# A gated MLP on one core of Trainium2: fifteen pairs of weight tiles by seven products in chains of up to five, and the norm's factor of the value side applied behind the output product

## The chip, the cores and the metric

The kernel runs on one core of a Trainium2 chip. The metric is the time of one execution on the device in microseconds (us); less is better. The engines of the core work in parallel, each on its own list of instructions: PE (TensorE) multiplies matrices into PSUM, DVE (VectorE), ACT (ScalarE) and POOL (GpSimd) work elementwise, and SP (SyncE) starts DMAs.

## What is computed

The model has two transformer blocks, 512 tokens of width 1024 and, in the first, 16 meta tokens more (528 columns). The first block has a layer of differential attention and one of latent attention, the second a mixer of a convolution and windowed attention. Each of these three layers is followed by a gated MLP, and the MLPs are what is changed:

```python
def conv_ffn(h, g_norm, w_in, conv_w, conv_b, w_out):
    L = h.shape[1]
    xn = rms_norm(h, g_norm)
    a, b = jnp.split(xn @ w_in, 2, axis=-1)
    ap = jnp.pad(a, ((0, 0), (CONV_W - 1, 0), (0, 0)))
    a_conv = conv_b
    for j in range(CONV_W):
        a_conv = a_conv + ap[:, j:j + L] * conv_w[j]
    return h + (jax.nn.silu(a_conv) * b) @ w_out
```

`rms_norm` multiplies each token by a factor R of its own, 1/sqrt(mean of squares + eps), and each channel by a gain. The MLP of the second block is the same in other names. The width between `w_in` and `w_out` is 2816, 22 tiles of 128. Everything is fp32.

## The kernel before

Activations lie transposed: channels on partitions, tokens along the columns. An fp32 operand is kept as a high and a low part of the type that PE multiplies, and a product is three matmuls: weight high by input high, weight high by input low, weight low by input high (`lin`, L329). The high part of weights is a cast on ACT (L162, `whi`), the low part a subtraction on DVE (L170) or, for some, on POOL (L112), both `wlo`. `Xh` and `Xl` are the parts of a layer's input `h` times its gain (L426 to L430), without R, which is a factor of a token and is applied behind the product.

**The MLP** (`ffn`, called three times; below MLP 1 to 3). Gate tile f and value tile NF+f make a pair. A pair runs in one of two ways. `Plain` makes both tiles by the 8 slices of the input's channels in two column halves: 2 x 8 x 2 x 3 = 96 matmuls. `Seven` makes the pair by seven products instead of eight, on sums and differences of halves of the weights and of the input: 7 blocks of 4 slices x 3 = 84 matmuls of H columns (264, 258 and 256 in MLP 1, 2 and 3). The sums of the input (`T`) are made once per MLP (`differences`), those of the weights for each pair by eight POOL additions of 128x256 (`combine`); they come from two loads (`raw`, `rawA`) and give four sets of weights, a, s, t and d. The sums overwrite `raw` and `rawA`, and the last set, d, is split from there by POOL, so that a buffer of `rawA` (two of them) is free for a later pair's load only when d is split.

Behind the products a pair goes on as follows. The gate side is multiplied by R, into `am` (L608 for a Plain; L672 for a Seven, whose sums go by L660, L666 and L670). `gate` does the convolution over three tokens (ACT, then two DVE instructions at L561) and SiLU, and **L565 multiplies the result by R**: that is R of the value side. L618 (Plain) or L678 (Seven) multiplies by the value product, and `split` puts the result as `Gh` and `Gl` into G.

**Groups.** The 22 pairs are taken in four groups (`GROUPS`: first pair, end, steps). A number among the steps is a Plain by itself; a tuple is a run of one or two Sevens whose products are mixed with those of the one Plain that stands last in it (`turns`). Per MLP that makes 12 Sevens and 10 Plains. After each group `group_h` multiplies the group's part of G by that part of `w_out`, for eight tiles `m` of output channels, and adds the result `po` to `h`: one DVE instruction that reads PSUM and SBUF (`add`, L693). MLP 1 does it in two column halves of 272 and 256, MLP 2 and 3 in one of 512. The last group's product leads into the next layer: `add_h` (L447) adds to `h`, takes the squares for the next norm (ACT into a ring of two buffers named `sq`, then sums `acc` and, behind MLP 2, `gacc`, on POOL but for the last), and makes `Xh` and `Xl` of the next layer. In MLP 3 `finish` does it, with the final norm and the output.

**What sets the order.** In `opening` (pair 0) and in the tuples PE's order is the order of the code (`in_order`). Otherwise, and on the other engines, a scheduler puts independent instructions in order when the program is built. Weights are taken from a plan (`plan_ffn`) in the order of use; `Weights.get` loads three sets ahead and splits two ahead. `tp` holds the working tiles of an MLP, `am` with two buffers, and six PSUM banks (`psp`) take the products.

## Time and profile before

| | |
|---|---|
| median of three runs | 2083.66 us (2083.62 to 2084.5) |
| the profiled execution | 2083.53 us, its span 2081.7 us |
| PE busy | 2041.2 us, 98% of the span |
| DVE busy | 1395.4 us, 67% |
| ACT busy | 975.1 us, 47% |
| POOL busy | 737.8 us, 35% |
| the chain that ended last | 82% PE, 12% DVE, 3% ACT |
| mean granted clock of TensorE | 0.995 of full speed |

The profile is of one execution. Its span runs from the first to the last recorded instruction; 1.8 us of the execution's time lie around it. "Busy" counts the time in which an engine works on at least one instruction; neighbouring DVE instructions overlap a little in the records, so that a mean duration is somewhat longer than the distance from start to start. The chain that ended last goes back from the last instruction to whatever released each step: where it runs through PE, matmuls took the time, where it runs through DVE, PE waited or would soon have waited for DVE.

### The profile page before, as it was taken

To read this page: it belongs to the slowest core of one execution; us is meant where nothing else is said; L and a number is where in the kernel's file an instruction comes from. 1 tells how busy PE (TensorE), PEld (TensorE's weight loads), DVE (VectorE), ACT (ScalarE), POOL (GpSimd) and SP (SyncE) were. 2 spreads that over 40 slices of the span, in tenths; PEclk is the share of its full clock that TensorE was granted. 3 is DMA by queue.
4 is the path that set the end of the run, shared out by engine and by line. 5 is a ranking of instruction groups with operands and counts; after the bars stand their busy time and mean duration, and the time that the engine had idled before them with its cause. 6 is when DMAs were issued, how large, how long until landed. Compare 5 with 4: busy or idle time off the path is not lost.

```text
span 2081.7 us, 36278 instructions
## 1 busy us (share of the span) xinstructions
PE 2041.2 (98%) x14327; PEld 1888.2 (91%) x14327; DVE 1395.4 (67%) x2536; ACT 975.1 (47%) x1940; POOL 737.8 (35%) x837
## 2 busy tenths in 40 slices
PE   8999999999999999999999999999999999999998
PEld 7999899999999989899899998788888889899997
DVE  8787769576767476658676768675533358577675
ACT  6565546344445455545344445354432235344444
POOL 5223243445343231124445453321122244435442
PEclk9999999999999999999999999999999999999999
DMA  5111132323322211022323323322223232323322
GB/s 170 52 54 59 42 103 76 97 86 104 102 79 82 68 41 42 31 88 73 114 80 104 93 94 93 92 81 78 70 76 102 97 117 69 104 85 108 112 71 72
DMA packets 56426, 174.91 MB, mean 84 GB/s; under 512 B 6464, under 2 KB 9408, under 8 KB 56256
## 3 DMA queue, kind: packets, MB, share of 16 engines
q1 hardware_dynamic: 55824, 172.34, 26.2%
q8 instruction: 112, 1.84, 0.4%
q14 instruction: 58, 0.48, 0.1%
q10 hardware_dynamic: 432, 0.27, 0.0%
HBM read 170.45 MB, written 2.10 MB: 83 GB/s over the span
## 4 chain that ended last, share of the span: by engine, by line
PE 82%; DVE 12%; ACT 3%; issue 1%; POOL 1%; DMA 1%; SPq 0%; ACTq 0%; DVEq 0%; POOLq 0%
PE po L329 22%; PE pf L552 17%; PE pf L329 13%; PE pc L329 5%; PE pq L329 5%; PE pg L329 4%; DVE wlo L170 3%; PE s L743 2%; PE pyc L329 2%; PE pm L329 2%; PE pd L329 2%; PE o L1383 1%; PE pya L329 1%; ACT whi L162 1%; PE pt L1361 1%
## 5 line engine op out<-in xcount | busy, mean ns | idle before, releaser
L162 ACT CAST whi<-raw 128x1024 fp32r<-128x1024 f32 (+4 forms) x460 | 382.0, 840 | 548.0 <-PE po L329 172.7
L112 POOL TENSOR_TENSOR wlo<-raw,whi 128x256 fp32r<-128x256 f32 (+1 forms) x336 | 291.9, 896 | 569.9 <-ACT whi L162 565.2
L170 DVE TENSOR_TENSOR wlo<-raw,whi 128x512 fp32r<-128x512 f32 (+2 forms) x580 | 398.6, 725 | 53.8 <-ACT whi L162 51.2
L329 PE MATMUL pf<-Xl,whi 128*128 128x256 f32 (+2 forms) x960 | 271.3, 283 | 0.9 <-DVE Xl L430 0.9
L329 PE MATMUL pf<-Xh,whi 128*128 128x256 f32 (+2 forms) x960 | 271.5, 283 | 0.0
L329 PE MATMUL pf<-Xh,wlo 128*128 128x256 f32 (+2 forms) x960 | 271.3, 283 | 0.0
L329 PE MATMUL po<-Gh,wlo 128*128 128x512 f32 (+2 forms) x709 | 238.8, 339 | 0.0
L329 PE MATMUL po<-Gl,whi 128*128 128x512 f32 (+2 forms) x709 | 238.5, 337 | 0.0
L329 PE MATMUL po<-Gh,whi 128*128 128x512 f32 (+2 forms) x709 | 235.7, 340 | 0.0
L329 PEld LDWEIGHTS pf<-Xl,whi 128*128 128x128 f32 x960 | 181.4, 189 | 1.2 <-DVE Xl L430 1.1
L329 PEld LDWEIGHTS pf<-Xh,whi 128*128 128x128 f32 x960 | 181.6, 189 | 0.0
L329 PEld LDWEIGHTS pf<-Xh,wlo 128*128 128x128 f32 x960 | 181.5, 189 | 0.0
L552 PE MATMUL pf<-Th,whi 128*128 128x264 f32 (+2 forms) x576 | 162.5, 282 | 0.3 <-DVE bm L666 0.3
L552 PE MATMUL pf<-Tl,whi 128*128 128x264 f32 (+2 forms) x576 | 162.3, 282 | 0.0
L552 PE MATMUL pf<-Th,wlo 128*128 128x264 f32 (+2 forms) x576 | 162.3, 282 | 0.0
L329 PEld LDWEIGHTS po<-Gh,wlo 128*128 128x128 f32 x709 | 133.2, 188 | 16.7
L329 PEld LDWEIGHTS po<-Gl,whi 128*128 128x128 f32 x709 | 133.4, 188 | 15.3
L329 PEld LDWEIGHTS po<-Gh,whi 128*128 128x128 f32 x709 | 132.4, 188 | 14.8
L693 DVE TENSOR_TENSOR h<-po,h 128x272 f32<-128x272 f32 (+1 forms) x96 | 53.6, 560 | 108.6 <-PE po L329 108.1
L552 PE MATMUL pf<-Xh,whi 128*128 128x264 f32 (+2 forms) x432 | 122.0, 282 | 2.6 <-DVE ct L618 2.6
L552 PE MATMUL pf<-Xh,wlo 128*128 128x264 f32 (+2 forms) x432 | 121.9, 282 | 0.0
L552 PE MATMUL pf<-Xl,whi 128*128 128x264 f32 (+2 forms) x432 | 121.8, 282 | 0.0
(425 smaller groups left out, 5568.8 us busy)
## 6 DMA issues: line engine op xcount, KB each, us to landing
raw<-in_w_in_dram SPq DMA_DIRECT2D x134, 512.0 KB, 3.6
raw<-in_w_up_dram SPq DMA_DIRECT2D x44, 512.0 KB, 3.3
raw<-in_w_qkv_dram SPq DMA_DIRECT2D x24, 512.0 KB, 3.6
raw<-in_w_out_dram SPq DMA_DIRECT2D x32, 384.0 KB, 3.1
raw<-in_w_out_dram SPq DMA_DIRECT2D x32, 320.0 KB, 2.9
raw<-in_w_o_dram SPq DMA_DIRECT2D x16, 512.0 KB, 3.4
raw<-in_w_dn_dram SPq DMA_DIRECT2D x16, 384.0 KB, 3.3
raw<-in_w_dn_dram SPq DMA_DIRECT2D x16, 320.0 KB, 2.9
```

The costliest lines, as they stand in the source:

```text
L112: self.net.nc.gpsimd.tensor_tensor(d[:, c], a[:, c], b[:, c], op=op)
L162: nc.scalar.copy(h[:, c0 : c0 + z], r)
L170: nc.vector.tensor_tensor(l[:, c], r[:, a:b], h[:, c].bitcast(F32), op=ALU.subtract)
L329: nc.tensor.matmul(ps, w, x, start=first and i == 0, stop=i == len(ops) - 1, skip_group_check=not first)
L552: nc.tensor.matmul(ps[:, :H], a, b, start=first and i == 0, stop=i == len(ops) - 1, skip_group_check=not first)
L693: nc.vector.tensor_tensor(self.h[:, m, s:e], p, self.h[:, m, s:e], op=ALU.add)
L743: nc.tensor.matmul(s[:, :w], qa[:, q0 : q0 + P], ka[:, k0:k1], start=z == 0, stop=z == len(ops) - 1 and not masked,)
L1361: nc.tensor.transpose(t[:, b * P : (b + 1) * P], p[:, j, a : a + P], self.ident)
L1383: nc.tensor.matmul(o[:, i, j, :], st[n, "pt", j][:, b * P : (b + 1) * P], V[:, b, c], start=n % 4 == j == b == 0, stop=False,)
```

## The change

There are two parts.

*Chains.* `GROUPS` now names for each group the single Plains ahead of it, the Sevens, and one Plain for the end. `chain` takes the place of `turns`: the first Seven's products 1, 5, 6, 2, then for each next Seven y, with x the one ahead of it, the order y1 x7 x3 y5 x4 y6 y2, and after the last the Plain, whose gate half is put around the last Seven's products 7, 3 and 4. Per MLP there are 15 Sevens and 7 Plains, in chains of 2, 4, 5 and 4 Sevens. `plan_ffn` follows that order, and the record of sums (`rows`) is kept by name, not in a queue.

*The factor R of the value side.* L565 goes. Since R belongs to a token, and a token is a column of the output product too, the output product is multiplied by it instead: in `add`, DVE writes `po` times R to a tile `pr` in the ring `am`, and POOL adds that to `h`; in `add_h` and `finish`, `scaled` writes it to a tile in the ring `sq`, and DVE adds it to `h`. R of the gate side stays where it was.

```diff
-    (0, 6, (0, 1, 2, (3, 4, 5))),
-    (6, 11, ((6, 7, 8), (9, 10))),
-    (11, 17, ((11, 12, 13), (14, 15, 16))),
-    (17, 22, ((17, 18, 19), (20, 21))),
+    (0, 6, (0, 1, 2), (3, 4), 5),
+    (6, 11, (), (6, 7, 8, 9), 10),
+    (11, 17, (), (11, 12, 13, 14, 15), 16),
+    (17, 22, (), (17, 18, 19, 20), 21),
 )
...
 
     def plan_ffn(self, wi, wo):
         pl = []
-        for k0, k1, steps in GROUPS:
-            for st in steps:
-                if isinstance(st, int):
-                    pl += [self.chunk(wi, st), self.chunk(wi, NF + st)]
-                    continue
-                *fs, g = st
-                a, d = [[self.chunk(wi, m + f)[1] for f in fs] for m in (0, NF)]
-                u = [
-                    [((wi, f, "a"), a[i] + d[i], 8, P, "a"), ((wi, f, "s"), [], 8, P, "s")]
-                    + [((wi, f, "t"), [], 8, P, "t"), ((wi, f, "d"), [], 4, P, "d")]
-                    for i, f in enumerate(fs)
-                ]
-                wa, wb = self.chunk(wi, g), self.chunk(wi, NF + g)
-                if len(u) == 1:
-                    pl += [*u[0][:2], wa, u[0][2], wb, u[0][3]]
-                else:
-                    pl += [*u[0][:2], wa, u[0][2], u[1][0], u[0][3], u[1][1], wb, *u[1][2:]]
+        for k0, k1, front, sevens, g in GROUPS:
+            pl += [self.chunk(wi, f + z) for f in front for z in (0, NF)]
+            units = [
+                [((wi, f, "a"), [self.chunk(wi, m)[1][0] for m in (f, NF + f)], 8, P, "a")]
+                + [((wi, f, c), [], 4 if c == "d" else 8, P, c) for c in "std"]
+                for f in sevens
+            ]
+            pl += units[0][:2]
+            for x, y in zip(units, units[1:]):
+                pl += [y[0], x[2], y[1], x[3]]
+            pl += [self.chunk(wi, g), *units[-1][2:], self.chunk(wi, NF + g)]
...
-    def add_h(self, ps, m, s, e, gain=None):
+    def add_h(self, ps, m, s, e, gain=None, R=None):
 
         nc = self.nc
         hs = self.h[:, m, s:e]
         last = m == KD - 1
+        ps = ps if R is None else self.scaled(ps, R[:, s:e])
         nc.vector.tensor_tensor(hs, ps, hs, op=ALU.add)
         self.sq_add(self.acc, hs, s, e, m == 0, last)
         if gain is not None:
...
         self.split(*self.X.at(m, s, e), self.h[:, m, s:e], g)
+
+    def scaled(self, ps, r):
+        t = self.nrm.tile([P, 512], F32, tag="sq", name=self.n("pr"))[:, : ps.shape[-1]]
+        self.nc.vector.tensor_tensor(t, ps, r, op=ALU.mult)
+        return t
 
     def begin_h(self, pool, tag, name, X, halves, m, hf, k0=0, k1=KD - 1):
 
...
                 nc.scalar.activation(t, t, AF.Silu)
-                nc.vector.tensor_tensor(t, t, R[:, t0:], op=ALU.mult)
                 return t
 
             def bank(first=False):
...
-            def turns(k0, *fs):
-
-                u = [Seven(f, f - k0) for f in fs[:-1]]
-                v = Plain(fs[-1], fs[-1] - k0)
-                x, y = u[0], u[-1]
-                x.p1(), x.p5(), v.a(0), x.p6(), x.p2(), v.a(1), x.p7()
-                if x is y:
-                    v.b(0), x.p3(), x.p4(), v.b(1)
-                    return
-                x.p3(), y.p1(), x.p4(), y.p5(), y.p6(), y.p2(), v.b(0), y.p7(), y.p3(), v.b(1), y.p4()
+            def chain(k0, fs, g):
+
+                u = [Seven(f, f - k0) for f in fs]
+                v = Plain(g, g - k0)
+                x = u[0]
+                x.p1(), x.p5(), x.p6(), x.p2()
+                for y in u[1:]:
+                    y.p1(), x.p7(), x.p3(), y.p5(), x.p4(), y.p6(), y.p2()
+                    x = y
+                v.a(0), x.p7(), x.p3(), v.a(1), x.p4(), v.b(0), v.b(1)
 
             def add(p, m, s, e):
-                nc.vector.tensor_tensor(self.h[:, m, s:e], p, self.h[:, m, s:e], op=ALU.add)
+                t = tp.tile([P, NT], F32, tag="am", name=self.n("pr"))[:, : e - s]
+                nc.vector.tensor_tensor(t, p, R[:, s:e], op=ALU.mult)
+                nc.gpsimd.tensor_tensor(self.h[:, m, s:e], t, self.h[:, m, s:e], op=ALU.add)
 
             R = self.nrm.tile([P, NT], F32, tag="R", name=self.n("R"), bufs=1)
             with self.in_order():
                 opening()
             differences()
-            for k0, k1, steps in GROUPS:
-                for st in steps:
-                    if st == 0:
-                        continue
-                    if isinstance(st, int):
-                        v = Plain(st, st - k0)
+            for k0, k1, front, sevens, g in GROUPS:
+                for f in front:
+                    if f:
+                        v = Plain(f, f - k0)
                         v.a(0, 2), v.b(0, 2)
-                    else:
-                        with self.in_order():
-                            turns(k0, *st)
+                with self.in_order():
+                    chain(k0, sevens, g)
                 if k1 < NF:
                     self.group_h(psp, wo, G, k0, k1 - k0, ranges, add)
             xcx.close()
             if nxt is None:
-                self.finish(psp, wo, G, k0, k1 - k0)
+                self.finish(psp, wo, G, k0, k1 - k0, R)
                 return
             nxt()
-            self.group_h(psp, wo, G, k0, k1 - k0, ranges, lambda p, m, s, e: self.add_h(p, m, s, e, gain))
+            self.group_h(psp, wo, G, k0, k1 - k0, ranges, lambda p, m, s, e: self.add_h(p, m, s, e, gain, R))
 
 
     def rope(self, dst, src, rows, C, S, mask, pool, s=0, e=NT):
...
                 hs = self.h[:, m, META:]
-                nc.vector.tensor_tensor(hs, ps, hs, op=ALU.add)
+                nc.vector.tensor_tensor(hs, self.scaled(ps, R[:, META:]), hs, op=ALU.add)
...
                 hs = self.h[:, m, s:e]
-                nc.vector.tensor_tensor(hs, ps, hs, op=ALU.add)
+                nc.vector.tensor_tensor(hs, self.scaled(ps, R[:, s:e]), hs, op=ALU.add)
```

Where the instructions stand now is seen in the order of each engine. **First, DVE behind the last group of MLP 1.** `h<-po` and, after the change, `pr<-po` and `h<-pr` are the adds, `Xl` the low part of the next layer's input, `wlo` the splitting of weights. Before:

```order
L447 TENSOR_TENSOR h<-po_8185,h 128x272 [waits PE_49]
L447 TENSOR_TENSOR h<-po_8186,h 128x256 [waits PE_49]
L447 TENSOR_TENSOR h<-po_8233,h 128x272 [waits PE_49]
L170 TENSOR_TENSOR wlo_8278<-raw_0_8231,whi_8277 128x320 [waits DMAHW1_49,Activation_49]
L170 TENSOR_TENSOR wlo_8278<-raw_0_8231,whi_8277 128x320
L447 TENSOR_TENSOR h<-po_8234,h 128x256 [waits PE_49]
L427 TENSOR_TENSOR Xl_8177<-h,Xh_8176 128x272 [waits DVE_49,Activation_49]
L447 TENSOR_TENSOR h<-po_8284,h 128x272 [waits PE_49]
L427 TENSOR_TENSOR Xl_8177<-h,Xh_8176 128x256 [waits DVE_49,Activation_49]
```

After:

```order
L453 TENSOR_TENSOR pr_8329<-po_8297,R_3999 128x272 [waits PE_49]
L453 TENSOR_TENSOR pr_8335<-po_8298,R_3999 128x256 [waits PE_49]
L442 TENSOR_TENSOR h<-pr_8329,h 128x272 [waits DVE_49]
L442 TENSOR_TENSOR h<-pr_8335,h 128x256 [waits DVE_49]
L170 TENSOR_TENSOR wlo_8397<-raw_0_8346,whi_8396 128x320 [waits DMAHW1_49,Activation_49]
L170 TENSOR_TENSOR wlo_8397<-raw_0_8346,whi_8396 128x320
L453 TENSOR_TENSOR pr_8380<-po_8348,R_3999 128x272 [waits DVE_49,PE_49]
L421 TENSOR_TENSOR Xl_8289<-h,Xh_8288 128x272 [waits Activation_49]
L421 TENSOR_TENSOR Xl_8289<-h,Xh_8288 128x256 [waits DVE_49,Activation_49]
L442 TENSOR_TENSOR h<-pr_8380,h 128x272 [waits DVE_49]
L453 TENSOR_TENSOR pr_8388<-po_8349,R_3999 128x256 [waits DVE_49,PE_49]
L442 TENSOR_TENSOR h<-pr_8388,h 128x256 [waits DVE_49]
```

Each add has become two instructions, a product with R from PSUM and an add of two SBUF tiles; the `Xl` of a tile stands behind both.

**Second, DVE behind the last group of MLP 2**, its last tiles. `acc` and `gacc` are the running sums of squares. Before:

```order
L447 TENSOR_TENSOR h<-po_15754,h 128x512 [waits PE_49]
L430 SCALAR_TENSOR_TENSOR Xl_15556<-h,gg,Xh_15555 128x512 [waits Activation_49]
L170 TENSOR_TENSOR wlo_15870<-raw_0_15784,whi_15869 128x512 [waits DMAHW4_49,Activation_49]
L170 TENSOR_TENSOR wlo_15870<-raw_0_15784,whi_15869 128x512
L430 SCALAR_TENSOR_TENSOR Xl_15556<-h,gg,Xh_15555 128x512 [waits Activation_49]
L447 TENSOR_TENSOR h<-po_15786,h 128x512 [waits PE_49]
L1662 CAST bandb<-band 128x256 [waits Pool_49]
L430 SCALAR_TENSOR_TENSOR Xl_15556<-h,gg,Xh_15555 128x512 [waits Activation_49]
L353 TENSOR_TENSOR acc<-acc,sq_15803 128x512 [waits Activation_49]
```

After (from three tiles ahead of the end):

```order
L453 TENSOR_TENSOR pr_15954<-po_15938,R_11977 128x512 [waits Pool_49]
L442 TENSOR_TENSOR h<-pr_15954,h 128x512 [waits DVE_49]
L424 SCALAR_TENSOR_TENSOR Xl_15762<-h,gg,Xh_15761 128x512 [waits DVE_49,Activation_49]
L453 TENSOR_TENSOR pr_15988<-po_15972,R_11977 128x512 [waits Pool_49]
L442 TENSOR_TENSOR h<-pr_15988,h 128x512 [waits DVE_49]
L424 SCALAR_TENSOR_TENSOR Xl_15762<-h,gg,Xh_15761 128x512 [waits DVE_49,Activation_49]
L453 TENSOR_TENSOR pr_16022<-po_16006,R_11977 128x512 [waits PE_49,Pool_49]
L442 TENSOR_TENSOR h<-pr_16022,h 128x512 [waits DVE_49]
L347 TENSOR_TENSOR acc<-acc,sq_16025 128x512 [waits Activation_49]
L347 TENSOR_TENSOR gacc<-gacc,sq_16028 128x512 [waits Activation_49,Pool_49]
L424 SCALAR_TENSOR_TENSOR Xl_15762<-h,gg,Xh_15761 128x512 [waits DVE_49,Activation_49]
```

The products with R wait for POOL (the ring `sq` that they share with the squares), and the last `Xl` has moved behind the last adds into `acc` and `gacc`.

**Third, POOL in the group from pair 11 on in MLP 1**, where weights of Sevens are summed. The number behind a name is that of the set of weights. `raw` and `rawS` are sums, `wlo` a split. Before:

```order
L112 TENSOR_TENSOR wlo89_6562<-raw84_1_6309,whi89_6561 128x256 [waits PE_49,Activation_49]
L112 TENSOR_TENSOR wlo89_6562<-raw84_1_6309,whi89_6561 128x256
L112 TENSOR_TENSOR raw90_0_6566<-raw90_0_6566 128x256 [waits Pool_49]
L112 TENSOR_TENSOR rawS94_6749<-raw94_1_6727 128x256 [waits DMAHW1_49]
L112 TENSOR_TENSOR rawS94_6749<-raw94_1_6727 128x256
L112 TENSOR_TENSOR raw94_1_6727<-raw94_0_6725,raw94_1_6727 128x256 [waits DMAHW0_49,Pool_49]
L112 TENSOR_TENSOR raw94_1_6727<-raw94_0_6725,raw94_1_6727 128x256 [waits Pool_49]
L112 TENSOR_TENSOR wlo95_6846<-raw90_1_6568,whi95_6845 128x256 [waits PE_49,Activation_49]
L112 TENSOR_TENSOR raw94_0_6725<-rawS94_6749,raw94_0_6725 128x256 [waits DVE_49,Pool_49]
```

After, inside the chain:

```order
L113 TENSOR_TENSOR wlo91_6592<-raw84_1_6306,whi91_6591 128x256 [waits PE_49,Activation_49]
L113 TENSOR_TENSOR wlo91_6592<-raw84_1_6306,whi91_6591 128x256
L113 TENSOR_TENSOR rawS92_6637<-raw92_1_6598 128x256 [waits DMAHW7_49,DVE_49]
L113 TENSOR_TENSOR rawS92_6637<-raw92_1_6598 128x256
L113 TENSOR_TENSOR raw92_1_6598<-raw92_0_6596,raw92_1_6598 128x256 [waits DMAHW5_49,DVE_49,Pool_49]
L113 TENSOR_TENSOR raw92_1_6598<-raw92_0_6596,raw92_1_6598 128x256 [waits Pool_49]
L113 TENSOR_TENSOR raw92_0_6596<-rawS92_6637,raw92_0_6596 128x256 [waits DVE_49,Pool_49]
L113 TENSOR_TENSOR raw92_0_6596<-rawS92_6637,raw92_0_6596 128x256 [waits Pool_49]
L113 TENSOR_TENSOR raw92_0_6596<-raw92_0_6596 128x256 [waits DVE_49,Pool_49]
```

Before, the splits of a Plain's or another set's weights lay between two Sevens' sums; now each Seven's eight sums stand directly behind the split of the d set (`wlo<-raw`) of the Seven two ahead of it, and wait for DMAs into the buffers that this split sets free.

## Rows read from the trace of the kernel before

**Rows 1.** The page, busy us of each engine (share of the span, instructions).
```profile
PE 2041.2 (98%) x14327; PEld 1888.2 (91%) x14327; DVE 1395.4 (67%) x2536; ACT 975.1 (47%) x1940; POOL 737.8 (35%) x837
```
**Rows 2.** Windows: length, then PE, PEld, DVE, ACT, POOL busy (instructions), clock, DMA, GB/s.
```profile
555.00:590.50 35.50, 35.50 (x293) 35.50 (x293) 18.36 (x33) 9.38 (x15) 13.04 (x16) 1.00 0.34 105
651.37:680.06 28.69, 28.68 (x236) 28.47 (x234) 28.03 (x73) 22.93 (x69) 12.91 (x15) 1.00 0.40 128
683.20:686.50 3.30, 3.30 (x17) 3.30 (x16) 0.90 (x4) 0.78 (x3) 0.00 (x0) 0.52 0.38 103
1277.90:1307.00 29.10, 26.63 (x110) 20.76 (x109) 28.48 (x35) 20.74 (x32) 20.86 (x18) 0.96 0.38 119
```
**Rows 3.** Windows over eleven stretches of 84 matmuls of one Seven: sum and mean.
```profile
sum 110.41, PE 110.41 PEld 110.41 DVE 103.05 ACT 76.56 POOL 52.96; mean PE 10.04 PEld 10.04 DVE 9.37 ACT 6.96 POOL 4.81
```
**Rows 4.** The chain that ended last: start, us, a run of matmuls (MLP 1, MLP 3).
```profile
352.49 10.15 PE pf L552 x84
...
1760.59 9.89 PE pf L552 x84
```
**Rows 5.** DVE by line and shape, 651.37:680.06: count, busy, mean ns; idle before.
```profile
L427 DVE TENSOR_TENSOR Xl<-h,Xh 128x256 fp32r<-128x256 f32 x8 | 4.3, 543 | 0.0
```
**Rows 6.** Timeline of DVE and POOL behind MLP 1: start, us, instruction [idle before].
```profile
667.38 0.99 DVE L427 TENSOR_TENSOR Xl<-h,Xh 128x256 fp32r<-128x256 f32 x1
...
672.42 0.42 DVE L427 TENSOR_TENSOR Xl<-h,Xh 128x256 fp32r<-128x256 f32 x1
672.76 0.42 DVE L447 TENSOR_TENSOR h<-po,h 128x256 f32<-128x256 f32 x1
...
666.42 1.66 POOL L353 TENSOR_TENSOR acc<-acc,sq 128x256 f32<-128x256 f32 x2 [1.52 <-ACT sq L351]
```
**Rows 7.** By line and shape, 1277.9:1307, DVE, POOL and ACT: columns as in Rows 5.
```profile
L430 DVE SCALAR_TENSOR_TENSOR Xl<-h,gg,Xh 128x512 fp32r<-128x512 f32 x8 | 11.6, 1465 | 0.6 <-ACT Xh L429 0.6
L170 DVE TENSOR_TENSOR wlo<-raw,whi 128x512 fp32r<-128x512 f32 x6 | 6.2, 1078 | 0.0
L447 DVE TENSOR_TENSOR h<-po,h 128x512 f32<-128x512 f32 x8 | 5.4, 674 | 0.0
...
L353 POOL TENSOR_TENSOR acc<-acc,sq 128x512 f32<-128x512 f32 x5 | 7.4, 1487 | 11.1 <-ACT sq L351 11.1
L353 POOL TENSOR_TENSOR gacc<-gacc,sq 128x512 f32<-128x512 f32 x4 | 6.6, 1660 | 0.9 <-ACT sq L351 0.9
L112 POOL TENSOR_TENSOR wlo<-raw,whi 128x256 fp32r<-128x256 f32 x6 | 5.8, 989 | 0.0
...
L351 ACT ACTIVATE sq<-h 128x512 f32<-128x512 f32 x6 | 3.7, 617 | 0.0
L351 ACT ACTIVATE sq<-h,par 128x512 f32<-128x512 f32 x5 | 3.6, 715 | 1.1 <-POOL gacc L353 1.1
```
**Rows 8.** The chain that ended last, behind MLP 2: the step of one add.
```profile
1279.98 0.60 DVE h L447
```
**Rows 9.** By line and shape, 491:590.5 in MLP 1, DVE and POOL: columns as in Rows 5.
```profile
L170 DVE TENSOR_TENSOR wlo<-raw,whi 128x512 fp32r<-128x512 f32 x26 | 19.0, 772 | 2.1 <-ACT whi L162 1.7
...
L565 DVE TENSOR_TENSOR ct<-ct,R 128x528 f32<-128x528 f32 x6 | 4.7, 775 | 1.9 <-ACT ct L564 1.9
...
L112 POOL TENSOR_TENSOR wlo<-raw,whi 128x256 fp32r<-128x256 f32 x18 | 17.8, 1015 | 17.7 <-ACT whi L162 17.7
L112 POOL TENSOR_TENSOR raw<-rawS,raw 128x256 f32<-128x256 f32 x8 | 7.6, 969 | 4.5 <-DVE wlo L170 4.5
...
L112 POOL TENSOR_TENSOR raw<-raw,raw 128x256 f32<-128x256 f32 x8 | 6.2, 791 | 15.0 <-DMA raw<-in_w_in_dram 15.0
```
**Rows 10.** Timeline of DVE in MLP 1: one split, POOL idle from 503.9 to 508.4.
```profile
504.38 0.68 DVE L170 TENSOR_TENSOR wlo<-raw,whi 128x512 fp32r<-128x512 f32 x1
```
**Rows 11.** Waits of PE over the whole execution: us in total, times, longest.
```profile
PE pf L552 <- DVE ct L618: 2.6, 2, 1.8
```
**Rows 12.** The page, DMA issues: KB each, median us from issue to landing.
```profile
raw<-in_w_in_dram SPq DMA_DIRECT2D x134, 512.0 KB, 3.6
```

21 lines of the change are left out of this document (10 added, 11 removed).

## The prediction

> **What bounds the kernel now.** I read the busy shares first: PE works 98% of the span, DVE 67%, POOL 35% [rows 1]. Then stretches of single stages. Inside the three MLPs PE has no gap at all: over an output product (the first of [rows 2]), and over eleven stretches in which one pair by seven products (a Seven, 84 matmuls) runs by itself [rows 3], PE is busy for the whole time. There a matmul taken away is time taken away. DVE is close behind, though: 9.37 of 10.04 us in the Seven stretches, with POOL at 4.81 beside it. Two stages are the other way round. After the last group of MLP 1 DVE is busy 28.03 of 28.69 us, and after that of MLP 2 28.48 of 29.10 [rows 2]; both are the exits, where DVE adds the product to `h`, makes the low half `Xl` of the next layer's input and splits weights. The next layer's first product needs the last `Xl`, so there DVE sets the time, and PE runs on at a granted clock of 0.52, the lower of its two levels (1.2 of 2.4 GHz), when it has stood waiting (the third of [rows 2]). So the change is weighed twice: PE's saving inside the MLPs, and DVE's added work at the exits.
>
> **What PE saves.** Nine of 66 pairs change from 96 matmuls to 84. The 84 take 10.15 us in MLP 1 and 9.89 in MLP 3 [rows 4], MLP 2 lies between; 12 matmuls are 1.45 to 1.41 us, nine times 1.43 is **-12.9 us**. All of it is in stretches where PE never waits, so it counts in full if nobody becomes late.
>
> **The exit of MLP 1.** The gate's multiplication by R goes, but 16 products with R are added where DVE has no room. A DVE instruction of this size takes 0.42 us, and the next starts 0.34 after it (second and third of [rows 6]): 16 x 0.35 = 5.6. The 16 adds into `h` now read two SBUF operands, not PSUM and SBUF, as the `Xl` subtraction does. That form takes 0.543 on average here against 0.42 undisturbed [rows 5, 6], because of POOL: at 667.38 it took 0.99 while POOL was running, at 672.42 0.42 while it was not [rows 6]; 16 x 0.12 = 1.9. In PE's order 42 matmuls of this product, not 56, stand ahead of the end of its first tile, 14 x 0.12 = 1.7 earlier. Nothing else of PE can fill in behind the last `Xl`. Together **+5.6 us** (3.9 with undisturbed adds; 8.0 if the adds stretch to 0.99 for the 45% of the time in which POOL runs, 16 x 0.45 x 0.57 = 4.1 in place of 1.9).
>
> The Trainium skill (GPSIMD Engine Reference, 1. Specifications) says that GpSimd shares its SBUF interfaces with VectorE and that the two contend when a DVE instruction has two SBUF inputs. By that rule the trace agrees, 0.99 against 0.42, and the rule speaks against this change: it turns PSUM-and-SBUF adds into SBUF-and-SBUF adds at the exits and gives POOL more work elsewhere. Without it the exit would be 3.9.
>
> **The exit of MLP 2.** Eight products 512 wide are added; DVE's step for this size is 0.60 [rows 8], so at least 4.8. But the products take tiles of the ring of two buffers in which the squares for POOL's two running sums lie, and from the third on they wait for POOL. Behind each stand DVE's add, the `Xl`, and the weights' splitting. Per tile three allocations now pass two buffers, so the next square for `acc` needs the buffer that POOL's `gacc` add frees. A lap is at least `gacc` 1.66 + square 0.62 + `acc` 1.49 = 3.8; POOL's other work of this stretch (six splits at 0.99 [rows 7], and what is left of its 20.86 [rows 2]) adds some 0.9 per lap, so 4.7. Seven laps are 33. After the last come product 0.6, add 0.67, squares 0.62 and 0.72, the `gacc` add 0.7, now ahead of the last `Xl` on DVE, and `Xl` 1.47: 4.8. That is 37.8 where 29.1 stood: **+8.7 us** (4.8 to 10.5).
>
> **The end.** MLP 3 goes out through `finish`, where one more DVE product stands in the last chain: 0.42 as in rows 6, **+0.5**.
>
> **The openings.** PE waits 2.6 us on `ct` of the first pairs [rows 11]. Three gate multiplications fewer stand ahead of that (3 x 0.775 per MLP, [rows 9]), so up to 2.6 can go. Against it, the first chain is (3,4) without a Plain in between and asks for its second unit 8.8 us sooner. Preparing a unit takes its load, 3.6 [rows 12], eight sums on POOL at 0.79 to 0.97 and two splits at 1.0 [rows 9], 9.1 in all: a loop of 12.7 where a unit lasts 10.0 on PE. One missed turn per MLP is 2.7, three 8. **-1 us** (-2.6 to +8); most of what PE waits for there is the differences and the splits, which stay.
>
> **The chains.** Two things decide whether PE stays without gaps in the nine chains.
> DVE: a unit costs 9.37 now [rows 3], less one R multiplication 8.6. POOL will be busy 9.1 of 10.0 us instead of 4.8. How far that stretches the eleven two-SBUF instructions of a unit is bounded by two rows of one and the same split: 0.68 with POOL idle [rows 10], 0.772 on average in these groups [rows 9], which carried on to 90% gives 0.07 more each, 0.8 per unit, 9.4 in all: no stall; and 1.078 at the exit with POOL at 72% [rows 2, 7], which gives 0.4 more each, 13.1 in all. I stay near the first, the same stage.
> POOL: the loop of 12.7 against 10.0 loses 2.7 per unit. A chain of five has a head start from the output product ahead of it (35.5 us, POOL busy 13.0 [rows 2], plus 16 new adds at 0.83 [rows 6], 13.3), and by my list of the loads and sums the last unit's fourth block is ready 0.5 us before it is asked for. So some of nine chains will stall a little, and each wait also costs low clock. **+3 us** (0 to +20).
> The product's adds on POOL inside the MLPs cost nothing as long as POOL's 26.3 us stay under 35.5: six PSUM banks and two `am` buffers lie between PE and it. DVE's products from the third on wait for POOL there, and the splits of output weights queue behind them; if that cover is gone, it costs what POOL is late, at most one add per group, 9 x 0.8 = 7, counted in the 20.
>
> **Sum.** -12.9 + 5.6 + 8.7 + 0.5 - 1 + 3 = +3.9. The profiled execution took 2083.53 (span 2081.7 and 1.8 around it), the median of the runs is 2083.66: 2085.6 + 1.8 + 0.1 = **2087.5 us**. PE's saving is eaten at the two exits.
>
> **Rivals.**
> *The saving stays.* The exits cost only their least (3.9 + 4.8 + 0.5), because POOL's ring is not what DVE waits for and the adds run at 0.42; chains without a stall; the openings give 1 to 2.6 back: -12.9 + 9.2 - 1 to -2.6 = -4.7 to -6.3, **2077.4 to 2079**. For it: the 0.42 in rows 6, and that POOL is idle 55% of MLP 1's exit. Against it: the products of MLP 2 that wait for POOL in DVE's order.
> *DVE and POOL stall PE in the chains* (slower than before). Place: from the third unit on, PE's fourth block waits for DVE's sum of the seventh product. It decides once a unit costs DVE more than PE by 0.5, since three periods then use up the 1.4 us that PE's order leaves. At 1.0 above (11.0, between 9.4 and 13.1) chains of four lose 1.6 and of five 2.6, 5.8 per MLP, 17 in all, in place of 3: **2101.5**. For it: MLP 2's split at 1.078. Against it: 0.772 in the groups themselves. It is the contention named beside rows 6, carried into the chains.
> *It does not do what it says*: nine Sevens could be spared 12 matmuls and PE not be shorter only if it waited; PE's list of instructions is 108 shorter, so this is no case of its own.
>
> **How the numbers follow.** Forecast 0.43, with a range of its own of 2081 to 2094; the saving stays 0.27; the chains stall 0.27; 0.03 for the rest, above. A measurement of this kernel can tell 0.2%, 4.2 us, from no change: faster is below 2079.5, slower above 2087.8. The first rival gives faster 0.24 and same 0.03, the forecast same 0.23 and slower 0.20, the second rival and the rest slower 0.30. So faster 0.24, same 0.26, slower 0.50. The range reaches to 2076.5 and 2104; beyond lie the openings' whole gain on one side, and a stretch nearer to 13.1 on the other, a tenth each.
>
> **What would show it.** PE busy should fall by some 13 us with no stretch of low clock inside the MLPs. From the first add of MLP 1's last product to its last `Xl` it should be about 36 us, not 28.7; MLP 2's 38, not 29. If those stretches keep their length, the forecast is wrong by up to 14 and the first rival holds; if PE waits for `bm` or for a fourth block's `wlo` inside chains, with DVE at over 95% there, the second does. It would also be wrong if the waits of DVE for POOL in the output products held PE's banks.

## The result and the profile after

The changed kernel takes 2117.77 us in the median of four runs (2114.55 to 2124.01), the kernel before, run beside it, 2083.64: a ratio of 1.0168 (95% interval 1.0148 to 1.0187). It is slower by 34 us, where the prediction had 2087.5 and a range that ended at 2104. Slower was the likeliest of its three outcomes (0.50); the size is outside the range.

The page of the changed kernel, busy shares and the chain that ended last (compare [rows 1]):

```profile
PE 2045.6 (97%) x14219; PEld 1883.7 (89%) x14219; DVE 1487.2 (70%) x2534; ACT 1000.8 (47%) x2012; POOL 939.8 (44%) x1015
...
PE 73%; DVE 13%; POOL 4%; ACT 4%; issue 3%; DMA 1%; ACTq 0%; SPq 0%; POOLq 0%; DVEq 0%
```

The 108 matmuls are gone, yet PE is busy no shorter (2045.6, before 2041.2), at a mean granted clock of 0.989 in place of 0.995. POOL has 202 us more to do, and DVE 92 us more, though its count fell by two: its instructions have become longer. The chain now runs through POOL and DMA for 5%, before for 2%; PE's part fell from 82% to 73%.

Cut at the first matmul of each stage, the two profiled executions (spans 2081.7 and 2112.8) differ so. "Without waits" scales the stage before by its matmuls. The row of either exit runs on through the next layer, up to that layer's own output product; these products and the first 24 matmuls of each opening, 137 us in both, are left out.

| stage | before | after | difference | of it waits |
|---|---|---|---|---|
| three groups of pairs 11 to 16 (now chains of five) | 189.6 | 207.8 | +18.2 | 22.5 (without waits 185.3) |
| six other groups from pair 6 on (now chains of four) | 318.8 | 314.1 | -4.7 | 3.9 (without waits 310.2) |
| openings, to the end of pair 5, three | 198.1 | 199.4 | +1.3 | |
| MLP 1's last product and the next layer | 251.0 | 256.9 | +5.9 | |
| MLP 2's last product and the next layer | 395.6 | 406.7 | +11.1 | |
| the end | 39.6 | 40.4 | +0.8 | |
| ahead of the first layer's output product | 262.2 | 260.4 | -1.8 | |

The output products inside the MLPs did not move (35.2 and 29.3 us in MLP 1, 33.6 and 28.0 in the others, as before). So the chains of five and the two exits carry the loss. These are single profiles: ahead of the first layer's output product, where nothing was changed, the profiles of the runs differ by some 4 us, and in the layer behind MLP 2's exit by up to 9. Measured from the product's first matmul to the last `Xl`, without the layer behind, MLP 1's exit grew from 35.8 to 40.6 us (+4.7) and MLP 2's from 38.8 to 51.4 (+12.6). Windows over the three stages of the first row in the kernel before (columns as in [rows 2]):

```profile
491.00:555.00 64.00, 64.00 (x530) 64.00 (x529) 49.57 (x78) 33.45 (x57) 32.42 (x35) 1.00 0.32 98
1118.30:1181.60 63.30, 63.30 (x530) 63.30 (x529) 50.17 (x80) 33.43 (x57) 33.94 (x35) 1.00 0.33 100
1894.30:1956.50 62.20, 62.20 (x529) 62.18 (x528) 50.50 (x77) 33.03 (x57) 36.01 (x37) 1.00 0.33 103
```

The same in the changed kernel:

```profile
488.50:555.50 67.00, 63.76 (x516) 62.92 (x515) 61.42 (x79) 36.99 (x67) 49.99 (x48) 1.00 0.34 107
1125.10:1194.90 69.80, 63.27 (x518) 62.24 (x517) 62.94 (x81) 37.76 (x68) 50.22 (x48) 1.00 0.34 103
1916.20:1987.10 70.90, 63.32 (x518) 62.31 (x517) 64.25 (x81) 37.70 (x69) 52.00 (x49) 0.98 0.33 101
```

PE had no gap before and now stands for 3 to 8 us in each, 17.4 in all. DVE is busy 90 to 92%, POOL 72 to 75%; neither is full, so shares alone don't name the cause. The waits of PE and the chain do. PE's waits over the whole execution:

```profile
PE pf L552 <- ACT u L653: 12.3, 6, 2.9
PE pf L552 <- DVE bm L665: 5.4, 5, 2.4
PE pc L323 <- ACT Xh L423: 5.3, 3, 3.6
...
PE pd L323 <- DVE Xl L421: 2.9, 2, 2.6
```

`u` at L653 is ACT's copy of a unit's products 1 and 6. ACT takes its instructions in order, and ahead of that copy stand casts (`whi`) whose raw weights come from POOL's sums. The chain of waits through MLP 2's chain of five shows it (start, us, what):

```profile
1143.05 2.31 POOL wlo L113 x2
1145.36 0.02 issue
1145.38 3.79 DMA raw<-in_w_in_dram
...
1150.26 1.18 POOL rawS L113
...
1152.55 1.24 POOL raw L113 x2
...
1156.91 2.30 POOL wlo L113 x2
1159.21 0.02 issue
1159.23 3.46 DMA raw<-in_w_in_dram
...
1162.82 0.37 POOL rawS L113
...
1168.84 0.03 ACT whi L162
...
1169.99 0.27 ACT u L653
```

Split of a fourth set (2.3), the load that takes its buffer (3.5 to 3.8), eight sums (7.7), the next split: from 1143.05 to 1156.91 it is 13.9 us for a unit that PE does in 10. The loop of the prediction (12.7) was there, longer by 1.2. In MLP 3 the chain runs the same way. In MLP 1, from 499 to 535, it runs through DVE for the most part, and PE's longest wait there, of the 3.2 us that it stands, is for DVE (the wait, then pieces of the chain):

```profile
PE pf L552 <- DVE bm L665: 2.4, 1, 2.4
...
509.49 0.34 DVE bm L665
...
521.24 0.34 DVE bm L665
...
534.49 0.35 DVE bm L665
```

From `bm` to `bm` DVE takes 11.75 us for a unit, then 13.25 (here it waited for casts of POOL's sums), where PE takes 10.15. So two loops are longer than PE's turn, POOL's and, by less, DVE's.

### The profile page after: what moved, and what is told of

It is laid out like the page before. It is cut to its first block, busy times and chain, and to the rows that moved or that the text cites. A ratio compares the mean times of both kernels' runs of the same rounds, so it can differ in the third digit from the quotient of the medians.

```text
span 2112.8 us, 36616 instructions
## 1 busy us (share of the span) xinstructions
PE 2045.6 (97%) x14219; PEld 1883.7 (89%) x14219; DVE 1487.2 (70%) x2534; ACT 1000.8 (47%) x2012; POOL 939.8 (44%) x1015
## 4 chain that ended last, share of the span: by engine, by line
PE 73%; DVE 13%; POOL 4%; ACT 4%; issue 3%; DMA 1%; ACTq 0%; SPq 0%; POOLq 0%; DVEq 0%
PE po L323 21%; PE pf L552 15%; PE pf L323 8%; PE pc L323 5%; PE pg L323 4%; PE pq L323 4%; DVE wlo L170 3%; PE s L741 2%; PE pyc L323 2%; POOL raw L113 2%; PE pm L323 2%; PE pd L323 1%; PE o L1381 1%; ACT whi L162 1%; PE pya L323 1%
## 5 line engine op out<-in xcount | busy, mean ns | idle before, releaser
L162 ACT CAST whi<-raw 128x1024 fp32r<-128x1024 f32 (+3 forms) x487 | 392.9, 821 | 599.7 <-PE po L323 193.9
L170 DVE TENSOR_TENSOR wlo<-raw,whi 128x512 fp32r<-128x512 f32 (+2 forms) x593 | 481.1, 849 | 57.1 <-ACT whi L162 53.6
L552 PE MATMUL pf<-Th,whi 128*128 128x264 f32 (+2 forms) x720 | 206.7, 287 | 22.5 <-ACT u L653 12.3
L323 PE MATMUL pf<-Xh,whi 128*128 128x256 f32 (+2 forms) x672 | 190.0, 283 | 1.1 <-DVE am L607 0.9
L323 PE MATMUL pf<-Xl,whi 128*128 128x256 f32 (+2 forms) x672 | 189.4, 282 | 0.9 <-DVE Xl L424 0.9
L323 PE MATMUL pf<-Xh,wlo 128*128 128x256 f32 (+2 forms) x672 | 189.3, 282 | 0.0
L552 PEld LDWEIGHTS pf<-Th,whi 128*128 128x128 f32 x720 | 136.1, 189 | 28.0 <-ACT u L653 14.2
L694 POOL TENSOR_TENSOR h<-pr,h 128x272 f32<-128x272 f32 (+1 forms) x96 | 115.2, 1207 | 79.4 <-DVE pr L693 79.4
L113 POOL TENSOR_TENSOR rawS<-raw 128x256 f32<-128x256 f32 x90 | 88.0, 996 | 125.8 <-DMA raw<-in_w_in_dram 66.7
L561 DVE SCALAR_TENSOR_TENSOR ct<-am,par,ct 128x512 f32<-128x512 f32 (+4 forms) x132 | 128.0, 971 | 12.3 <-ACT ct L557 10.7
```

The source lines that it names most:

```text
L113: self.net.nc.gpsimd.tensor_tensor(d[:, c], a[:, c], b[:, c], op=op)
L162: nc.scalar.copy(h[:, c0 : c0 + z], r)
L170: nc.vector.tensor_tensor(l[:, c], r[:, a:b], h[:, c].bitcast(F32), op=ALU.subtract)
L323: nc.tensor.matmul(ps, w, x, start=first and i == 0, stop=i == len(ops) - 1, skip_group_check=not first)
L552: nc.tensor.matmul(ps[:, :H], a, b, start=first and i == 0, stop=i == len(ops) - 1, skip_group_check=not first)
L561: nc.vector.scalar_tensor_tensor(t[:, z:], am[:, a : a + n - z], w, t[:, z:], op0=ALU.mult, op1=ALU.add)
```

## The experiments

All runs stand beside runs of the kernel before on the same chip; times are medians, the ratio is to the kernel before, with its 95% interval. Stages are from one profile of each run. "Chains of five" is the sum of their three stages in the profile, 207.8 us in the changed kernel. Its line is the sum of the windows over the three.

### The two parts of the change, each alone

Chains without the move of R (`add`, `add_h` and `finish` as before):

```diff
                 nc.scalar.activation(t, t, AF.Silu)
+                nc.vector.tensor_tensor(t, t, R[:, t0:], op=ALU.mult)
```

> The chains of the changed kernel, but R of the value side back in the gate and the adds into h as before (one DVE instruction from PSUM, no adds on POOL). Theory A (the loop over a pair's raw weights: load, eight sums on POOL, split of the fourth set, next load, some 13.9 us a unit against 10 on PE, with the head start that POOL has at a chain's start): the exits give back 18 us and POOL is free at the start of each chain, so the stalls in the three chains of five fall from 22 us to about 8: 2083.6 - 12.9 + 8 = 2079 (2073 to 2085). Theory B (DVE at over 90% in a chain, stretched by POOL): a unit costs DVE 0.78 more again, so the stalls grow to 30: 2101.

2102.65 us, ratio 1.0097 (1.0082 to 1.0113). The total is theory B's, the stages are neither's: the chains of five take 200.7, a stall of 15.4, not 8 and not 30. So with DVE's product back in the gate and no adds on POOL two thirds of the stall remain. The rest of the loss lies in the openings, 6.7 us longer than before, and in the stage of MLP 2's exit, 400.0 (4.4 longer); the exit itself is not the cause, as its last `Xl` comes 38.3 us after the product's first matmul, before 38.8. MLP 1's is back at 249.6. The windows over the chains of five, summed:

```profile
sum 200.72, PE 189.19 PEld 187.51 DVE 178.94 ACT 109.71 POOL 125.12; mean PE 63.06 PEld 62.50 DVE 59.65 ACT 36.57 POOL 41.71
```

The move of R without the chains, on the `GROUPS` and `turns` of before:

```diff
                 nc.scalar.activation(t, t, AF.Silu)
-                nc.vector.tensor_tensor(t, t, R[:, t0:], op=ALU.mult)
```

> The kernel before with the move of R alone (products with R behind the output product, adds on POOL), 12 units by seven products as before. If the exits cost what the profile of the changed kernel shows (5.9 + 11.1 + 1.0) and chains of at most two units don't stall: 2083.6 + 18 = 2101.6 (2099 to 2105). If the move's cost at the exits came from the chains: about 2084.

2097.87 us, ratio 1.0080 (1.0065 to 1.0095): as expected of the exits (258.6, 407.6, end 42.3). Its openings are 5.3 us shorter than before, its inner groups the same within 0.6 each. The losses of the two parts, 21 and 16, add up to 37 where both together lost 34. The stages don't add up like that: the chains of five stall for 15.4 us with the chains alone and for 22.5 with both, so the move of R costs some 7 us there, while MLP 2's exit stage is 5 us shorter than the sum of its two (4.4 and 12.0 against 11.1).

### What stalls a chain of five

One unit less in the third groups:

```diff
-    (11, 17, (), (11, 12, 13, 14, 15), 16),
+    (11, 17, (11,), (12, 13, 14, 15), 16),
```

> The changed kernel, with pair 11 of the third group made the plain way, so that no chain has more than four units by seven products (14 per MLP in place of 15). Theory A (the loop over raw weights uses up its head start after four units): the stalls of 22 us in the chains of five go, three pairs cost 4.3 us more on PE: 2117.8 - 22 + 4 = 2100 (2098 to 2105). Theory B (DVE is late in every period of a chain): a chain loses a quarter of its stalls: 2117.8 - 5.6 + 4.3 = 2116.5.

2099.01 us, ratio 1.0086 (1.0071 to 1.0101). Those stages fall to 191.8 us with 36 matmuls more, a stall of 2.2: the fourth unit is still in time, the fifth is not. Pair 11, now a Plain ahead of the chain, also gives POOL more time for the first sums. But the six chains of four of the changed kernel have no such Plain, and they stall for 3.9 us in all.

Two sums less per unit (the last of the four sums of the weights is left out):

```diff
-        self.sums(a[0][:, hi], a[0][:, hi], a[0][:, lo], ALU.subtract)
```

> The changed kernel, leaving out the last two of the eight POOL sums of each unit (the last sum of the weights isn't made, so the values are others). The loop over raw weights is 2.4 us shorter per unit. Theory A: a chain of five is ready some four times 2.4 us earlier, the stalls of 22 us go almost wholly: 2117.8 - 20 = 2098 (2095 to 2102). Theory B: POOL's share falls from 0.9 to 0.7 and DVE's stretch by a quarter: 2110.

2092.50 us, ratio 1.0048 (1.0032 to 1.0065). The chains of five take 191.6, the stall falls from 22.5 to 6.3, and the chains of four gain too.

Some 0.7 us less of DVE's work per unit (the gate side's product with R is left out in the Sevens):

```diff
-                    nc.vector.tensor_tensor(a, a, R[:, a0:], op=ALU.mult)
```

> The changed kernel, leaving out the gate side's product with R in every unit by seven products (the values are others): DVE has 0.73 us less per unit, POOL has the same work. Theory A (POOL's loop): the chains of five stay within 1 us each, 2117.8 - 2 = 2116. Theory B (DVE is late in every period): 0.73 x 4 less per chain of five and what it stretches POOL, 10 in all: 2107.

2113.72 us, ratio 1.0154 (1.0137 to 1.0171). The chains of five stay at 206.7, though DVE has 13.6 us less to do in them. PE's gaps do shrink, from 17.4 to 12.5 us (length less PE busy), but its matmuls take 3.9 us longer: the mean granted clock in the three chains is 0.95 to 0.97, in the changed kernel 0.98 to 1.00. Why it fell there is not shown.

```profile
490.33:558.05 67.72, 65.23 (x518) 64.64 (x517) 57.07 (x75) 36.88 (x67) 48.54 (x48) 0.97 0.34 106
1127.76:1199.01 71.25, 65.59 (x517) 64.87 (x516) 58.64 (x76) 37.59 (x68) 48.26 (x48) 0.95 0.33 101
1917.55:1985.32 67.77, 63.40 (x517) 62.58 (x516) 59.28 (x76) 37.40 (x68) 49.22 (x49) 0.97 0.33 106
```

The windows over the three chains, summed, with two POOL sums less per unit:

```profile
sum 191.58, PE 187.09 PEld 185.94 DVE 176.15 ACT 111.91 POOL 121.24; mean PE 62.36 PEld 61.98 DVE 58.72 ACT 37.30 POOL 40.41
```

And with the product with R left out:

```profile
sum 206.74, PE 194.22 PEld 192.09 DVE 175.00 ACT 111.87 POOL 146.03; mean PE 64.74 PEld 64.03 DVE 58.33 ACT 37.29 POOL 48.68
```

DVE is equally loaded in both, 176 and 175; POOL has 25 us less to do in the first, and the time differs by 15, PE's gaps by 8 (4.5 and 12.5). So POOL's sums are the first cause. DVE is the second: less work for it took 4.8 us off PE's gaps. The runs can't tell how much of the gain from fewer sums is POOL's own loop and how much is that DVE, in fewer conflicts with POOL, had 12 us less to do (188.6 in the changed kernel, 176 here); but the same relief of DVE alone changed the time by only 1 us, which speaks for the loop as the larger part.

The adds inside the MLPs on DVE in place of POOL:

```diff
-                nc.gpsimd.tensor_tensor(self.h[:, m, s:e], t, self.h[:, m, s:e], op=ALU.add)
+                nc.vector.tensor_tensor(self.h[:, m, s:e], t, self.h[:, m, s:e], op=ALU.add)
```

> The changed kernel with the add into h inside the MLPs on DVE in place of POOL (16 or 8 per output product); the exits are as in the changed kernel. Theory A with the head start: POOL can make the sums of the first units while PE multiplies by the output weights, and the chains of five in MLP 2 and 3 fall by 3 each to the 67 us that the run with R back in the gate has, MLP 1's stays at 67: 2117.8 - 6 = 2112. If the adds on POOL delay nothing: 2115 to 2119. If DVE's adds make DVE late there: above 2120.

2110.47 us, ratio 1.0136 (1.0123 to 1.0149): 7 us back, as the head start asks. The chains of five fall by 4.7 to 203.1, in MLP 2 and 3 by 1.2 and 4.0, while MLP 1's stays. PE's gaps in them fall by 7.5, to 9.9, and its matmuls take 2.9 longer:

```profile
sum 203.10, PE 193.20 PEld 191.47 DVE 179.79 ACT 112.36 POOL 130.38; mean PE 64.40 PEld 63.83 DVE 59.93 ACT 37.45 POOL 43.46
```

The output products are no longer than before, so DVE has the room. Why POOL's adds take the head start is on the page of the changed kernel:

```profile
L694 POOL TENSOR_TENSOR h<-pr,h 128x272 f32<-128x272 f32 (+1 forms) x96 | 115.2, 1207 | 79.4 <-DVE pr L693 79.4
```

POOL stood 79.4 us in all ahead of these adds, waiting for DVE's products, with sums of the next chain behind them in its order. The prediction had counted that time as free. The head start is a part of the stall, though, not the whole: without these adds it is still 17.8 us, and 15.4 in the run of the chains alone.

A third buffer for `rawA`, so that the load need not wait for the split. It was paid for with one `rawS` in place of two and two `ct` in place of three, so it stands beside its control, which has the smaller rings and two `rawA`:

```diff
-            t = pool.tile([P, 1024], F32, tag=tag, name=f"raw{self.nl}_{i}")
+            t = pool.tile([P, 1024], F32, tag=tag, name=f"raw{self.nl}_{i}", **({"bufs": 3} if i else {}))
```

> The changed kernel with three buffers in place of two for the second raw tile of a unit (rawA), paid for with one rawS in place of two and two ct in place of three. A unit's load no longer waits for the split of the fourth set two units ahead. Theory A1 (the loop is load 3.5 + sums 9.4 + split 2.3 at POOL's 1.18 us a sum, and the load is the part that can be taken out): a unit takes 11.8 in place of 13.9, and the chains of five lose 2.1 less per turn over three turns, 6 each: 2117.8 - 16 = 2102 (2097 to 2106). Theory A2 (POOL's own work, 11.8 of 10 us a unit, is the bound, and the load lies beside it anyway): the same time, 2115 to 2120. Theory B (DVE): the same time as well.

> The control to the run with three rawA: the changed kernel with one rawS and two ct, and two rawA as ever. If the third rawA took load time out of the loop (theory A1), this one is slower than that run's 2145.8, by some 16: 2162. If POOL's own work and not the load is the bound (A2), it is the same, 2143 to 2149, and the 28 us that run lost are the price of the single rawS and the two ct.

2145.76 us, ratio 1.0303 (1.0287 to 1.0318), and the control 2146.44, 1.0309 (1.0291 to 1.0327). The 28 us are the price of the smaller rings. In time the third buffer brings nothing, but not in each stage. Chains of five with it, windows summed:

```profile
sum 209.35, PE 192.44 PEld 189.34 DVE 184.63 ACT 110.17 POOL 155.22; mean PE 64.15 PEld 63.11 DVE 61.54 ACT 36.72 POOL 51.74
```

And in the control:

```profile
sum 217.01, PE 195.83 PEld 192.35 DVE 183.95 ACT 111.08 POOL 152.65; mean PE 65.28 PEld 64.12 DVE 61.32 ACT 37.03 POOL 50.88
```

They are 7.7 us shorter, 4.3 of it in PE's gaps, so the load's wait seems to be a part of the loop; the chains of four and the stage of MLP 2's exit are longer by 3.2 and 2.7. How much the load alone would give with the rings as they were stays open.

### What the exits cost

The product with R in place in PSUM:

```diff
-        t = self.nrm.tile([P, 512], F32, tag="sq", name=self.n("pr"))[:, : ps.shape[-1]]
-        self.nc.vector.tensor_tensor(t, ps, r, op=ALU.mult)
-        return t
+        self.nc.vector.tensor_tensor(ps, ps, r, op=ALU.mult)
+        return ps
```

> The changed kernel, where the exits' product with R is written in place in PSUM, so that it takes no tile of the ring of squares and the add into h reads PSUM again. If the ring and the adds with two SBUF operands made part of the exits' cost: MLP 2's exit costs only DVE's 8 products, 5 in place of 11, MLP 1's 4 in place of 6: 2117.8 - 8 = 2110. If DVE's added instructions are the whole cost (16 x 0.35 and 8 x 0.6 and what the squares wait anyway): 2115 to 2119.

2107.69 us, ratio 1.0115 (1.0096 to 1.0134). The stage of MLP 2's exit falls from 406.7 to 395.0, before's 395.6; MLP 1's stays at 257.2. Without the layer behind, MLP 2's last `Xl` ends 51.4 us after the product's first matmul in the changed kernel, 41.1 here, and 38.3 in the run of the chains alone, which has the same order of pairs and no products with R at the exit. So the larger part of the cost there, 10.4 us, goes with the ring of squares and what the waits on it made of the order; the eight products on DVE still cost 2.8. DVE of the changed kernel from the first product to the last `Xl`, in the middle three instructions per tile and then a wait:

```profile
1287.95 0.69 DVE L453 TENSOR_TENSOR pr<-po,R 128x512 f32<-128x512 f32 x1 [1.17 <-PE po L323]
...
1311.10 0.68 DVE L453 TENSOR_TENSOR pr<-po,R 128x512 f32<-128x512 f32 x1
1311.82 1.07 DVE L442 TENSOR_TENSOR h<-pr,h 128x512 f32<-128x512 f32 x1
1314.87 1.25 DVE L424 SCALAR_TENSOR_TENSOR Xl<-h,gg,Xh 128x512 fp32r<-128x512 f32 x1 [1.98 <-ACT Xh L423]
1317.30 0.69 DVE L453 TENSOR_TENSOR pr<-po,R 128x512 f32<-128x512 f32 x1 [1.17 <-POOL acc L347]
1318.02 1.01 DVE L442 TENSOR_TENSOR h<-pr,h 128x512 f32<-128x512 f32 x1
1321.02 1.87 DVE L424 SCALAR_TENSOR_TENSOR Xl<-h,gg,Xh 128x512 fp32r<-128x512 f32 x1 [1.98 <-ACT Xh L423]
...
1331.45 0.75 DVE L424 SCALAR_TENSOR_TENSOR Xl<-h,gg,Xh 128x512 fp32r<-128x512 f32 x1
```

The last laps from `pr` to `pr` are 5.2 to 6.2 us, and DVE idles 2 us in the last three for `Xh`, which ACT makes behind two squares: in DVE's order the next product stands behind the `Xl`, as it waits for a buffer that POOL sets free. With the product in PSUM DVE keeps on, busy 33.04 of the 35.45 us from its first product on (a window):

```profile
1295.95:1331.40 35.45, 33.90 (x143) 26.08 (x142) 33.04 (x43) 21.85 (x34) 25.66 (x21) 1.00 0.36 113
```

In its timeline the next product follows the add without a wait, and the last `Xl` ends at 1329.83:

```profile
1319.82 0.68 DVE L442 TENSOR_TENSOR h<-po,h 128x512 f32<-128x512 f32 x1
1320.42 0.69 DVE L452 TENSOR_TENSOR po<-po,R 128x512 f32<-128x512 f32 x1
...
1328.14 1.69 DVE L424 SCALAR_TENSOR_TENSOR Xl<-h,gg,Xh 128x512 fp32r<-128x512 f32 x1 [0.79 <-ACT Xh L423]
```

That the stage is no longer than before, though the last `Xl` ends 2.3 us later (41.1 after 38.8), goes with PE's clock behind the exit: in the 25 us from the next layer's first matmul on the mean granted clock, between its two levels of 1.2 and 2.4 GHz, was 0.93 before, 0.73 in the changed kernel, where PE stood waiting for `Xh` and `Xl` for 7 of them, and 1.00 here (the three in this order):

```profile
1296.20:1321.20 25.00, 22.53 (x98) 17.95 (x97) 15.93 (x22) 10.97 (x15) 13.38 (x12) 0.93 0.39 123
1308.80:1333.80 25.00, 17.75 (x54) 11.90 (x53) 14.60 (x17) 9.79 (x16) 14.43 (x12) 0.73 0.18 62
1316.80:1341.80 25.00, 23.45 (x107) 18.18 (x106) 18.20 (x28) 9.79 (x13) 13.44 (x13) 1.00 0.37 115
```

The run changes two things at once, the ring and the add's second SBUF operand; no run takes them apart. The adds were 0.787 on average with the tile in SBUF and 0.680 from PSUM, 8 x 0.1, so the ring has most of the 10.4 us. In MLP 1 the last `Xl` comes 1.3 us earlier than in the changed kernel (39.3 after 40.6; 36.7 in the run of the chains alone); the layer behind took 1.7 longer, so that the stage does not show it.

R moved in the first three groups alone, with the `GROUPS` of before, the last group's product with R back in the gate:

```diff
+                if f >= GROUPS[-1][0]:
+                    nc.vector.tensor_tensor(t, t, R[:, t0:], op=ALU.mult)
```

> The kernel before with the move of R in the first three groups of each MLP only: the last group's gates keep their product with R and the exits are as before; 12 units by seven products in the order of before. From the run with the move of R alone, whose openings were 3.8 us shorter and whose other inner stages were at most 1 longer: 2081.7 - 3 = 2079 (2077 to 2080.5). If the shorter openings came from something else than R, or the adds on POOL cost what DVE gains: 2081 to 2084.

2080.35 us, ratio 0.9990 (0.9981 to 1.0000): 17.5 less than the move in all groups, and 2.4 less than the kernel before beside it, at the edge of what can be told.

### A version that beats both

The order of before in the first and third groups, chains of four in the second and fourth, R behind the product wherever that was free (`late` is true in MLP 2 and 3, whose exits multiply in PSUM):

```diff
+    (0, 6, (0, 1, 2, (3, 4, 5))),
+    (6, 11, ((6, 7, 8, 9, 10),)),
+    (11, 17, ((11, 12, 13), (14, 15, 16))),
+    (17, 22, ((17, 18, 19, 20, 21),)),
...
+                if not late and f >= GROUPS[-1][0]:
+                    nc.vector.tensor_tensor(t, t, R[:, t0:], op=ALU.mult)
```

> What the runs so far leave worth having, together: chains of four in the second and fourth group, the order of before in the first and third (14 units by seven products per MLP); R of the value side behind the product in the first three groups, in MLP 2 and 3 in the last one too, there in place in PSUM; in MLP 1 the last group's gates keep their product with R. From the stages of the runs: 2080.4 of the run with R in the inner groups alone, less 2.3 (chains of four in the second groups), less 2.4 (in the fourth), less 3.4 (exit of MLP 2 as with the product in PSUM), plus 0.4 at the end: 2072.7 (2070 to 2077), 0.4% faster than before. If the stages don't add up, since a chain of four takes the head start of what stands behind it: 2077 to 2082.

2077.09 us, ratio 0.9975 (0.9965 to 0.9985): a quarter of a percent faster than the kernel before. It is less than the sum of its parts: MLP 2's exit came as expected (395.4), the openings are 5.3 shorter than before, but the six groups with chains of four take 318.7 us, before's 318.8, though they hold 72 matmuls fewer. So the Sevens in them should earn nothing:

```diff
-    (6, 11, ((6, 7, 8, 9, 10),)),
+    (6, 11, ((6, 7, 8), (9, 10))),
...
-    (17, 22, ((17, 18, 19, 20, 21),)),
+    (17, 22, ((17, 18, 19), (20, 21))),
```

> The mixed kernel with the second and fourth groups in the order of before as well (12 units by seven products per MLP, 72 more matmuls on PE): only the move of R is left, behind the product in the inner groups, in PSUM at MLP 2's and 3's ends, in the gate in MLP 1's last group. In the mixed kernel's profile the six groups with chains of four sum to the same time as before (318.7 against 318.8 us), so chains of four earn nothing: 2077 (2075 to 2079). If the 72 matmuls count: 2077.1 + 8.7 = 2085.8.

2079.49 us, ratio 0.9983 (0.9975 to 0.9992). The two intervals overlap: between the medians lie 2.4 us, where the 72 matmuls are 8.7 us of PE's work. This version has nothing but the move of R, so that alone is worth 0.17% over before, where it frees DVE and costs little.

## Why the prediction was wrong

**PE's saving, -12.9.** Right as a count: 8.6 in the chains of four and 4.3 in those of five. But "it counts in full if nobody becomes late" was the condition, and it failed: 26.4 us of new waits lie in the same stages.

**The chains, +3 (0 to +20).** This is the step that failed: 26.4, of it 22.5 in three stages. The loop was sized at 12.7 and measured 13.9 (sums 7.7, two splits 2.3, load 3.8). The greater error is the next sentence, that the last unit's fourth block "is ready 0.5 us before it is asked for". It took POOL's free time in the output product (35.5 less 26.3) as a head start. POOL takes its list in order, and the new adds, each waiting for DVE and PE, stand between the sums. The run with the adds on DVE gives 4.7 us of it back, 7.5 of PE's gaps. The rest is there without any adds on POOL (15.4 in the run of the chains alone) and is mainly the loop: a fifth unit falls behind (four units: 2.2), and six sums in place of eight hold it (6.3). The cap of 20 came without a working of its own. The prediction's own 2.7 per unit, over the two or three units without a head start, in three chains, is 16 to 24; with the measured 3.9 it is 23 to 35.

**The rival that stalls the chains** (0.27, 2101.5) had the right place and sign, and named the engine that comes second: it took DVE's stretch for the cause. The stretch is real: the split takes 1.078 in MLP 2's chain of five, the far end of the prediction's two bounds, and took 0.827 in that stage before (before, then after):

```profile
L170 DVE TENSOR_TENSOR wlo<-raw,whi 128x512 fp32r<-128x512 f32 x20 | 15.9, 827 | 1.6 <-ACT whi L162 1.5
L170 DVE TENSOR_TENSOR wlo<-raw,whi 128x512 fp32r<-128x512 f32 x25 | 26.2, 1078 | 6.0 <-ACT whi L162 5.9
```

The Trainium skill (GPSIMD Engine Reference, 1. Specifications) names that contention for DVE instructions with two SBUF inputs, and the trace agrees, 1.078 after 0.827. Less work for DVE moved the chains by 1 us (PE's gaps by 4.8), and less for POOL by 16 (PE's gaps by 12.9). In MLP 1's chain of five DVE was the first to be late all the same, at 11.75 us a unit; that is the rival's condition, a unit that costs DVE more than PE by 0.5, though DVE was busy 90 to 92% in the three chains and not over 95%. It was late elsewhere too: in the run of the chains alone PE waited for `bm` twelve times, 6.7 us, and with three `rawA` and the smaller rings 19.5.

**MLP 1's exit, +5.6.** The stage is +5.9, of it 4.7 up to the last `Xl`; the number is right, partly by luck. From the first product with R to the last `Xl` it is 35.2 us ("about 36"), with DVE busy 34.14, so the place and the engine were right. The terms were sized 5.6 for the products, 1.9 for the adds' second SBUF operand and -1.7 for the first tile (which make 5.8). The runs show 2.5 for the products, 1.3 for the second operand and the ring together, and +0.9 for the new order of pairs, though the first tile did come 1.7 earlier.

```profile
648.95:684.16 35.21, 31.92 (x248) 31.20 (x247) 34.14 (x89) 22.62 (x68) 13.34 (x15) 0.95 0.39 119
```

**MLP 2's exit, +8.7 (4.8 to 10.5).** The stage is +11.1, just beyond its bound (+12.6 up to the last `Xl`, 1.5 less behind it), by the mechanism that was named, the ring; but the ring was sized too small. From the first product to the last `Xl` 44.2 us were measured, not 37.8: seven laps took 40.0, not 33. Their length runs through ACT's `Xh` and DVE's idle 2 us, not through POOL's work alone. "At least 4.8" for the eight products was too much: with the ring out of the way they cost 2.8.

**The openings, -1.** +1.3: the 5.3 us that the move of R gives there (the run of R alone) were taken back by the first chain, 6.7 in the run of the chains alone. That this is since it asks sooner for its second unit is likely, as with six sums in place of eight the openings are 4.1 us shorter, but no run shows it by itself. The end: +0.8 in place of 0.5.

The forecast itself lay within its own bounds of no change; only its chances leaned to slower. Without the 26.4 us of waits in the chains the kernel would still have been slower by some 8 us, mostly at the exits. The size was wrong mainly because of one term, the chains, and the range left it out.

## What to carry to other kernels

When a change makes one engine's work shorter and gives a loop across other engines more turns in a row, compare the loop's period with the bound engine's time per turn: a period that is longer by 3.9 us can cost that much per turn once the buffers ahead are used up (3 to 8 us of gaps per chain of five here), whatever the busy shares say (POOL 72 to 75%, DVE 90 to 92%). Free time of an engine that takes its list in order is no head start while instructions that wait stand ahead in the list. And a new temporary in an existing ring is not free (some 10 us here): look at who else takes tiles of that ring, and whether the result could stay where it is, here in PSUM.
